# Output projections of tiles 3 and 4: input rows of the norm loaded one step ahead, first convolution rows into the weights' buffer

## The chip, the cores and the metric

The kernel runs on one core of one Trainium2 chip. TensorE (PE) multiplies matrices; VectorE (DVE) and ScalarE (ACT) do elementwise work, GpSimd (POOL) a little of it; SyncE (SP) issues most DMA transfers, ACT some. Engines run their own queues in order and wait for each other by semaphores. The metric is the device time of one execution in microseconds, and a kernel's time is the median of several runs.

## The reference, cut to what matters

One decoder layer on x (1 x 2048 x 1024, float32):

```python
hn = rms_norm(h, mix_pre_g)                  # h = x
proj = hn @ w_in
attn_out = sliding_window_attention(q, k, v, attn_sinks, rel_bias)   # window 128
conv_out = conformer_conv(u, ...)            # GLU, 31 taps, LayerNorm, swish, pointwise
mixed = jnp.concatenate([attn_out, conv_out], axis=-1) @ w_out
h = h + rms_norm(mixed, mix_post_g)          # output projection and its norm
hn = rms_norm(h, ffn_pre_g)
ff = (jax.nn.silu(hn @ w_gate) * (hn @ w_up)) @ w_down               # D_FF = 2816
h = h + rms_norm(ff, ffn_post_g)
```

The change lies in the fifth to seventh of these lines: the product with `w_out`, the norm behind it, the addition of the input x, and the norm ahead of the FFN.

## The kernel before, in words

Tokens are worked in four tiles of T = 512 (w = 0 to 3; "tiles 3 and 4" are w = 2 and 3). Float32 accuracy comes from splitting each operand into a high and a low part and multiplying three times; a split is one ACT copy and one DVE subtraction. Names in the trace are `tag@stage`: `ql@W` is a tile from the pool with tag `ql`, used in stage W. Stages of one letter with the tile's number: A input projection, B attention, C convolution, W output projection, N the norm behind W where it is a step of its own, H and F the FFN's gate and up projections (operands and products), G the FFN's down projection. F0 and G0 serve tiles 1 and 2 together, F2 and G2 tiles 3 and 4. The FFN uses a Strassen-like scheme: seven types of products, eleven pairs of blocks each, so G0 is 7 x 11 x 12 = 924 matmuls.

The program is built stage by stage, and a scheduler then orders each engine's queue. To fill gaps, stages run beside each other in lanes (generators that yield between portions of work). Beside G0 run, in this order: C2 (the convolution of tile 3), W2, C3, W3, and N3, the norm of W3; a second lane finishes the first FFN half. Then comes F2.

Every tag has a fixed number of buffers; a new tile waits until the oldest with that tag is no longer read or written. What matters here:

```python
BUFS = dict(x=4, p=4, wx=1, gb=2, hl=8, ql=4, chl=5, mid=4, mb=2, fa=4, at=2, fc=3, glu=2, yt=1, raw=2, w=6, vd=2)
```

`wx` is one buffer of 128 x 1024 float32, which early stages use for weights, the norm for a row block of x, and the finishing of the FFN (`ht`, L1149) for rows of h. `mid` has four buffers: the accumulators of W2 and W3 (`acc`), and later four operands of F2 (`mid@H`, split by ACT at L870 and DVE).

`stage_w` (from L723) is the output projection of one tile. It takes the eight blocks of `mixT` (attention and convolution results, transposed) in groups of two: `load(gi)` issues their DMAs (L749), `acts` splits them into `ql` (ACT L738, then DVE), `weight` loads and splits the weights (`w@W`, `raw@W`), and `block_half` multiplies (`tr@W`) and sums into `acc`. The first group is loaded when the stage begins. For tiles 3 and 4 blocks go to the two `at` buffers, that of w = 1 to a spare tile, and of w = 0 to `fa`.

`norm_w` (from L775) follows: squares of the four row blocks (s = 0 to 3), a factor by `rsqrt` (the `sm@W` chain), then per row block the scaling by factor and gain (`post_scale`, two DVE instructions per block, `mid@W<-mid@W,sm@W,gb@W`), the load of x rows (L798 into `wx` for one block, L804 in two halves for the others), the addition, the store of h to `h_scr` (L806) and the square (ACT L807). After the second factor ACT scales the blocks (L814) and stores them to `hn_scr` (L817). F2 reads columns of `hn_scr` back, transposes them (`tr@H`, L847) and splits them.

In G0 each step loads one operand (`fa@G` from `mids`, L1176; `at@G` in the first two steps) and one weight block (`mb@G`), splits both (`hl@G`, ACT L829 and DVE), and multiplies (`mm@G`). At the end of a type the sums leave PSUM through `p@G` (L1207, L1209), `mm@G` (L1249) and `x@G`.

Of the kernel before, what the change touches and what calls it, by code (L numbers as in the profile page):

```python
# [18 lines left out]
ALU = mybir.AluOpType  # L19
# [4 lines left out]
D = 1024  # L24
DFF = 2816
P = 128
T = 512
# [10 lines left out]
def layer_kernel(ctx, tc, x, xT, cols, rows, sinks, relb, onehot, w_in, w_pw, w_out, w_gate, w_up, w_down, out):  # L38
    nc = tc.nc
# [7 lines left out]
    lab = ["X0"]  # L47

    def nm(s):
        uid[0] += 1  # L50
        return f"{s}@{lab[0]}_{uid[0]}"
# [3 lines left out]
    def t_(tag, shape, dt=F32):  # L55
        return sb.tile(list(shape), dt, tag=tag, name=nm(tag), bufs=BUFS[tag])

    def f4(tag, shape=(P, D)):
        return t_(tag, shape)

    def f2(tag, shape=(P, T)):
        return t_(tag, shape)

    def hl(tag):
        return t_(tag, (P, 2, T), F32R)

    def sm(n, dt=F32):
        kind = "A" if lab[0][0] == "G" else lab[0][0]
        return sb.tile([P, 8], dt, tag="sm" + kind, name=nm("sm"), bufs={"C": 8, "W": 4}.get(kind, 16))[:, 0:n]
# [13 lines left out]
    def dve(op):  # L83
        def emit(*args, **kw):
            r = op(*args, **kw)  # L85
            if not paced[0]:
                pace["main"] = r.ins
            elif pace["main"] is not None and pace["main"] is not pace["tied"]:
                tc.add_manual_dep(
                    r.ins,  # L90
                    pace["main"].name,
                    mybir.DependencyInfo(mybir.DependencyClass.NoSync, mybir.DependencyReason.DATA),
                    reason="conv taps keep pace with the projections",
                )
                pace["tied"] = pace["main"]
            return r

        return emit

    stt = dve(nc.vector.scalar_tensor_tensor)  # L100
    vtt = dve(nc.vector.tensor_tensor)
# [38 lines left out]
    def weight(src, low, made, raw=None, on_pool=True):  # L140
        if raw is None:
            raw = t_("raw", (P, 2, T))
            nc.sync.dma_start(raw, src)
        return [split_w(raw[:, n], "w", low[n], made, on_pool) for n in range(2)]
# [5 lines left out]
    def rsqrt(ssq, n, mean_over, beside_taps=True):  # L150
        v = sm(n)
        y = sm(n)
        t = sm(n)
        vts(v, ssq, 1.0 / mean_over, EPS, ALU.mult, ALU.add)
        vts(y.bitcast(I32), v.bitcast(I32), 1, None, ALU.logical_shift_right)
        vts(y.bitcast(I32), y.bitcast(I32), -1, 0x5F3759DF, ALU.mult, ALU.add)
        for _ in range(3):
            if beside_taps:
                ptt(t, y, y, ALU.mult)
                ptt(t, t, v, ALU.mult)  # L160
                nc.gpsimd.tensor_scalar(t, t, -0.5, 1.5, ALU.mult, ALU.add)
                ptt(y, t, y, ALU.mult)
            else:
                vtt(t, y, y, ALU.mult)
                stt(t, v, -0.5, t, ALU.mult, ALU.mult)
                stt(y, t, 1.5, y, ALU.add, ALU.mult)
        return y
# [38 lines left out]
    for i in range(4):  # L206
        xt = f4("x", (P, 2, T))
# [415 lines left out]
    def spare_tile():  # L623
        if not spare:
            spare.append(t_("mb", (P, 2, T)))
        return spare[0]
# [76 lines left out]
    def block_half(acc, units, n, first, L, bank_of, s0=0):  # L703
        cs = slice(n * T, (n + 1) * T)
        for i in range(len(acc)):
            s = i + s0
            lab[0] = L
            o = bank_of()
            three(o, [((a[s // 4][:, 0, ss(s)], a[s // 4][:, 1, ss(s)]), (w[:, 0], w[:, 1])) for a, w in units])
            if first:  # L710
                act(acc[i][:, cs], o, AF.Copy)
            else:
                vtt(acc[i][:, cs], acc[i][:, cs], o, ALU.add)
            yield 0.65 * len(units)

    def load_gb(row):
        gb = []
        for n in range(2):
            t = f2("gb")
            nc.sync.dma_start(t, rows[row, n * T : (n + 1) * T].partition_broadcast(P))  # L720
            gb.append(t)
        return gb

    def post_scale(acc, gb, r):
        for n in range(2):
            cs = slice(n * T, (n + 1) * T)
            tied(stt(acc[:, cs], acc[:, cs], r, gb[n], ALU.mult, ALU.mult))

    def stage_w(w, spill, G, atag, htag, mtag, bank_of, norm=None):
        L = f"W{w}"  # L730
        lab[0] = L
        acc = [f4(atag) for _ in range(4)]

        def acts(gi, ms=None):
            aa = []
            for m in ms or load(gi):
                a = hl(htag)
                act(a[:, 0], m, AF.Copy)  # L738
                vtt(a[:, 1], m, a[:, 0].bitcast(F32), ALU.subtract)
                aa.append([a])  # L740
            return aa

        stage = spare_tile() if w == 1 else None

        def load(gi):
            ms = []
            for c in range(G * gi, G * gi + G):
                ms.append(stage[:, c % 2] if w == 1 else f2(mtag))
                nc.sync.dma_start(ms[-1], mixT[c, :, w * T : (w + 1) * T])  # L749
            return ms  # L750

        first = load(0)
        gb = load_gb(0) if w > 1 else None
        if w != 1:
            yield 5.0 if w == 0 else 8.0
            lab[0] = L
        nxt = acts(0, first)
        for gi in range(KC // G):
            aa = nxt
            for n in range(2):  # L760
                lab[0] = L
                if n == 0 and gi + 1 < KC // G:
                    if w < 2 and G * gi + G == 4:
                        ld.until(f"C{w}")
                        lab[0] = L
                    rows_next = load(gi + 1)
                if n == 1 and gi + 1 < KC // G:
                    nxt = acts(gi + 1, rows_next)
                src = w_out[2 * gi : 2 * gi + 2] if gi < 2 else w_join[2 * gi - 4 : 2 * gi - 2]
                ws = weight(src[:, :, n * T : (n + 1) * T].rearrange("c p t -> p c t"),  # L770
                            lo_out[n, 2 * gi : 2 * gi + 2], w > 0)
                yield from block_half(acc, list(zip(aa, ws)), n, gi == 0, L, bank_of)
        tail = norm_w(w, spill, acc, mtag, gb)
        if norm:
            norm(tail)  # L775
        else:
            yield from tail

    def norm_w(w, spill, acc, mtag, gb):
        L = f"W{w}"  # L780
        lab[0] = L
        gb = gb or load_gb(0)
        ssq = sm(4)
        for s in range(4):
            act(junk, acc[s], AF.Square, accum_out=ssq[:, s : s + 1])
            yield 0.5
            lab[0] = L
        r = rsqrt(ssq, 4, D, w < 3)
        yield 3
        lab[0] = L  # L790
        ssq2 = sm(4)
        for s in range(4):
            lab[0] = L
            post_scale(acc[s], gb, r[:, s : s + 1])
            r0 = w * T + s * P
            if s == (2 if mtag == "fa" else 0):
                xt = f4("wx")
                nc.sync.dma_start(xt, x[r0 : r0 + P])  # L798
                vtt(acc[s], xt, acc[s], ALU.add)
            else:  # L800
                for n in range(2):
                    cs = slice(n * T, (n + 1) * T)
                    xt = f2(mtag if s == 1 or w > 1 else "fa")
                    nc.sync.dma_start(xt, x[r0 : r0 + P, cs])  # L804
                    vtt(acc[s][:, cs], xt, acc[s][:, cs], ALU.add)
            nc.sync.dma_start(h_scr[r0 : r0 + P], acc[s])  # L806
            act(junk, acc[s], AF.Square, accum_out=ssq2[:, s : s + 1])  # L807
            yield 5.0
        lab[0] = L
        r2 = rsqrt(ssq2, 4, D, w < 3)  # L810
        yield 3
        lab[0] = L
        for s in range(4):
            act(acc[s], acc[s], AF.Copy, scale=r2[:, s : s + 1])  # L814
            if spill:
                r0 = w * T + s * P
                nc.scalar.dma_start(hn_scr[r0 : r0 + P], acc[s])  # L817
        yield 0.1
        hns[w] = acc
# [727 lines left out]
```

## Time and profile before

| | |
| --- | --- |
| times of three runs, us | 1981.5, 1977.93, 1981.22 |
| median, us | 1981.22 |
| profiled execution, us | 1986.73 |
| its span, us | 1984.7 |
| mean granted clock of TensorE in it | 0.992 |
| instructions | 26851 |

The profile is of one execution, which was 5.5 us over the median; its span is 2 us shorter than its own device time. The trace gives each instruction its start, its duration and, in square brackets, the engine's idle time before it with what ended that. In rows of groups, three durations are minimum, median and maximum in ns.

### The profile page before, as it was taken

Reading aid. Unit: us, or ns where it says so; the run is one execution under the profiler, and the core shown is the slowest. Engines: PE = TensorE matmul, PEld = TensorE weight load, DVE = VectorE, ACT = ScalarE, POOL = GpSimd, SP = SyncE. Lnnn points to the kernel's source line nnn. Section 1 sums busy time; section 2 is a strip of 40 time slices with the busy share of each in tenths; the row PEclk is TensorE's granted clock in tenths of the full one; section 3 lists DMA queues with packets and bytes.
Section 4 is the critical chain, followed back from the end, with each engine's and each line's share of the span. In section 5 each row is a group of like instructions: output and inputs, shape, how many; then the busy total and the mean of one; then the engine's idle time right before and its main releaser. Section 6 shows DMA issues by size and latency. Waiting matters only on the chain.

```text
span 1984.7 us, 26851 instructions
## 1 busy us (share of the span) xinstructions
PE 1937.4 (98%) x8730; PEld 1545.6 (78%) x8730; DVE 1493.7 (75%) x2679; ACT 969.5 (49%) x1910; POOL 335.2 (17%) x395
## 2 busy tenths in 40 slices
PE   9999999999999999989999999999999999999998
PEld 7877667677768878768878878777888888888886
DVE  5998989697793899888748995688766665455557
ACT  5455334546576633333345446477544433345443
POOL 6001212331120300000000011005423332311000
PEclk9999999999999999999999999999999999999999
DMA  8886646568758676686577778679745442366654
GB/s 313 275 308 224 203 149 186 181 193 305 270 166 303 224 252 223 230 275 233 193 241 252 226 270 276 215 291 345 265 142 176 170 153 91 136 224 202 212 190 155
DMA packets 229181, 443.56 MB, mean 223 GB/s; under 512 B 22920, under 2 KB 48688, under 8 KB 229040
## 3 DMA queue, kind: packets, MB, share of 16 engines
q1 hardware_dynamic: 207408, 406.19, 61.0%
q10 hardware_dynamic: 19392, 28.32, 3.9%
q0 software_dynamic: 2240, 7.34, 0.9%
q8 instruction: 68, 1.11, 0.2%
q14 instruction: 73, 0.60, 0.1%
HBM read 320.64 MB, written 121.12 MB: 223 GB/s over the span
## 4 chain that ended last, share of the span: by engine, by line
PE 77%; DVE 8%; DMA 8%; ACT 3%; issue 2%; POOL 1%; SPq 0%; ACTq 0%; DVEq 0%; POOLq 0%
PE mm@F L108 36%; PE mm@G L108 16%; PE mm@A L108 12%; PE mm@W L108 4%; PE tr@W L108 3%; PE tr@B L108 3%; DVE fc@C L85 3%; PE ct@J L108 1%; DMA raw@A<-w_in 1%; DVE mid@W L85 1%; DMA at@W<-mixT 1%; DMA gb@F<-keeps 1%; DMA mids<-fa@F 1%; DVE w@F L85 1%; DMA mixT<-fc@C 1%
## 5 line engine op out<-in xcount | busy, mean ns | idle before, releaser
L85 DVE SCALAR_TENSOR_TENSOR fc@C<-glu@C,colt,fc@C 128x512 f32<-128x512 f32 x480 | 365.9, 778 | 2.2
L108 PE MATMUL mm@F<-hl@H,w@F 128*128 128x512 f32 x1056 | 257.6, 392 | 3.5 <-ACT mm@F L983 3.5
L108 PEld LDWEIGHTS mm@F<-hl@H,w@F 128*128 128x128 f32 x1056 | 198.7, 189 | 48.4 <-ACT mm@F L983 4.8
L108 PE MATMUL mm@G<-hl@G,hl@G 128*128 128x512 f32 x924 | 226.0, 395 | 6.6 <-ACT mm@G L1249 2.2
L108 PE MATMUL mm@A<-hl@A,w@A 128*128 128x512 f32 x840 | 209.3, 399 | 2.1 <-DVE hl@A L85 1.1
L108 PEld LDWEIGHTS mm@G<-hl@G,hl@G 128*128 128x128 f32 x924 | 172.3, 189 | 45.5 <-ACT mm@G L1249 2.6
L108 PE MATMUL mm@G<-w@G,hl@G 128*128 128x512 f32 x876 | 199.5, 389 | 0.0
L829 ACT ACTIVATE w@F<-chl@F 128x512 fp32r<-128x512 f32 x220 | 134.7, 624 | 126.4 <-PE mm@F L108 119.3
L108 PEld LDWEIGHTS mm@G<-w@G,hl@G 128*128 128x128 f32 x876 | 164.4, 188 | 34.1
L108 PEld LDWEIGHTS mm@A<-hl@A,w@A 128*128 128x128 f32 x840 | 156.8, 190 | 40.6 <-issue 3.6
L85 DVE TENSOR_TENSOR w@F<-chl@F,w@F 128x512 fp32r<-128x512 f32 x198 | 143.3, 728 | 36.9 <-ACT w@F L829 36.4
L108 PE MATMUL mm@F<-ql@H,w@F 128*128 128x512 f32 x528 | 131.3, 392 | 7.2 <-ACT mm@F L1071 3.7
L108 PE MATMUL mm@F<-mid@H,w@F 128*128 128x512 f32 x528 | 131.3, 391 | 2.8 <-ACT fa@F L1092 2.6
L108 PE MATMUL mm@F<-p@H,w@F 128*128 128x512 f32 x528 | 131.2, 394 | 0.0
L108 PE MATMUL mm@F<-x@H,w@F 128*128 128x512 f32 x528 | 127.5, 390 | 0.0
L108 PEld LDWEIGHTS mm@F<-ql@H,w@F 128*128 128x128 f32 x528 | 98.6, 188 | 28.6 <-ACT mm@F L1071 4.6
L108 PEld LDWEIGHTS mm@F<-mid@H,w@F 128*128 128x128 f32 x528 | 98.6, 188 | 24.9 <-ACT fa@F L1092 3.5
L108 PEld LDWEIGHTS mm@F<-p@H,w@F 128*128 128x128 f32 x528 | 100.7, 191 | 21.6 <-ACT at@F L1085 0.3
L108 PEld LDWEIGHTS mm@F<-x@H,w@F 128*128 128x128 f32 x528 | 98.6, 188 | 21.3 <-DVE sm@B L460 0.8
L133 ACT ACTIVATE w@A<-raw@A 128x512 fp32r<-128x512 f32 x110 | 67.4, 626 | 77.4 <-PE mm@A L108 42.9
L108 PE MATMUL mm@W<-w@W,hl@W 128*128 128x512 f32 x384 | 103.2, 408 | 1.6 <-ACT fa@A L355 1.6
L85 DVE TENSOR_TENSOR w@G<-raw@G,w@G 128x512 fp32r<-128x512 f32 x73 | 51.5, 705 | 67.7 <-ACT w@G L829 66.7
(308 smaller groups left out, 3313.9 us busy)
## 6 DMA issues: line engine op xcount, KB each, us to landing
mids<-fa@F SPq DMA_DIRECT2D x154, 256.0 KB, 2.8
raw@A<-w_in SPq DMA_DIRECT2D x55, 512.0 KB, 4.7
w@A<-lo_in SPq DMA_DIRECT2D x84, 256.0 KB, 3.7
fc@G<-mids SPq DMA_DIRECT2D x77, 256.0 KB, 3.3
fa@G<-mids SPq DMA_DIRECT2D x75, 256.0 KB, 5.0
w@W<-lo_out SPq DMA_DIRECT2D x48, 256.0 KB, 4.1
chl@F<-w_gate SPq DMA_DIRECT2D x22, 512.0 KB, 4.2
raw@F<-w_gate SPq DMA_DIRECT2D x22, 512.0 KB, 3.7
```

What stands on the lines that cost most here:

```text
L85: r = op(*args, **kw)
L108: r = nc.tensor.matmul(*args, **kw)
L133: act(w[:, 0], raw, AF.Copy)
L829: act(w[:, 0], x, AF.Copy)
```

## The change

In `load`, the first group of tiles 3 and 4 (w > 1, gi = 0) goes into one tile of tag `wx`, shared by its two blocks, instead of two `at` tiles.

In `norm_w`, the loads of x rows move into a helper, `load_x_rows(s)`. For tiles 3 and 4 the rows of blocks 0 (in `wx`) and 1 (in `at`) are loaded ahead of the loop over the row blocks, and those of block s + 1 at the end of step s, from step 1 on. For tiles 1 and 2 a block's rows are loaded where they were. The addition of the block in `wx`, one DVE instruction over 1024 columns, becomes two over 512 in all four tiles.

```diff
         def load(gi):
             ms = []
+            pair_ = stage if w == 1 else t_("wx", (P, 2, T)) if w > 1 and gi == 0 else None
             for c in range(G * gi, G * gi + G):
-                ms.append(stage[:, c % 2] if w == 1 else f2(mtag))
+                ms.append(pair_[:, c % 2] if pair_ is not None else f2(mtag))
                 nc.sync.dma_start(ms[-1], mixT[c, :, w * T : (w + 1) * T])
             return ms
...
         r = rsqrt(ssq, 4, D, w < 3)
+        rows_x = {}
+
+        def load_x_rows(s):
+            if s < 4:
+                lab[0] = L
+                r0 = w * T + s * P
+                rows_x[s] = []
+                if s == (2 if mtag == "fa" else 0):
+                    xt = f4("wx")
+                    nc.sync.dma_start(xt, x[r0 : r0 + P])
+                    rows_x[s] = [xt[:, 0:T], xt[:, T:D]]
+                    return
+                for n in range(2):
+                    xt = f2(mtag if s == 1 or w > 1 else "fa")
+                    nc.sync.dma_start(xt, x[r0 : r0 + P, n * T : (n + 1) * T])
+                    rows_x[s].append(xt)
+
+        if w > 1:
+            load_x_rows(0)
+            load_x_rows(1)
         yield 3
...
             post_scale(acc[s], gb, r[:, s : s + 1])
             r0 = w * T + s * P
-            if s == (2 if mtag == "fa" else 0):
-                xt = f4("wx")
-                nc.sync.dma_start(xt, x[r0 : r0 + P])
-                vtt(acc[s], xt, acc[s], ALU.add)
-            else:
-                for n in range(2):
-                    cs = slice(n * T, (n + 1) * T)
-                    xt = f2(mtag if s == 1 or w > 1 else "fa")
-                    nc.sync.dma_start(xt, x[r0 : r0 + P, cs])
-                    vtt(acc[s][:, cs], xt, acc[s][:, cs], ALU.add)
+            if w < 2:
+                load_x_rows(s)
+            for n in range(2):
+                cs = slice(n * T, (n + 1) * T)
+                vtt(acc[s][:, cs], rows_x[s][n], acc[s][:, cs], ALU.add)
             nc.sync.dma_start(h_scr[r0 : r0 + P], acc[s])
             act(junk, acc[s], AF.Square, accum_out=ssq2[:, s : s + 1])
+            if w > 1 and s:
+                load_x_rows(s + 1)
             yield 5.0
```

Lines below the helper move down by 18 in the changed kernel (L829 becomes L847, L1176 becomes L1194). The counts of matmuls, ACT instructions and DMAs stay; DVE has four instructions more. The scheduler's order differs only in W0 and W1 (the two halves of one addition each) and from the end of F0 through G0 to the first products of F2, where all engines' queues are reordered around W2, C3, W3 and N3.

## The prediction

> **What bounds the kernel now.** I read the page first (span, busy times, the chain that ended last), then PE's busy time by stretches of 50 us where the change acts, then PE's waits in those 400 us, then the order of events around each wait. From the page:
>
> ```profile
> span 1984.7 us, 26851 instructions
> PE 1937.4 (98%) x8730; PEld 1545.6 (78%) x8730; DVE 1493.7 (75%) x2679; ACT 969.5 (49%) x1910; POOL 335.2 (17%) x395
> PE 77%; DVE 8%; DMA 8%; ACT 3%; issue 2%; POOL 1%; SPq 0%; ACTq 0%; DVEq 0%; POOLq 0%
> ```
>
> TensorE works for 98% of the span, and the change adds and removes no matmul. It can only create or remove idle time of PE. Outside the output projections of tiles 3 and 4 (labels W2 and W3), the instruction order of the changed kernel is that of before, but for two additions. W2 and W3 run beside G0, the down projection of tiles 1 and 2, from 1015 to 1340 us, so I asked for PE's time from 1000 to 1400 (the sum of eight windows) and for its waits there (total us, times, longest):
>
> ```profile
> sum 400.00, PE 389.27 PEld 317.76 DVE 311.61 ACT 233.50 POOL 54.65; mean PE 48.66 PEld 39.72 DVE 38.95 ACT 29.19 POOL 6.83
> PE tr@W L108 <- ACT ql@W L738: 2.5, 1, 2.5
> PE mm@G L108 <- ACT mm@G L1249: 2.2, 1, 2.2
> PE mm@G L108 <- DVE p@G L1209: 1.7, 1, 1.7
> PE tr@H L847 <- issue: 1.6, 1, 1.6
> PE mm@G L108 <- DVE x@G L85: 1.4, 1, 1.4
> PE mm@G L108 <- DVE hl@G L85: 0.7, 1, 0.7
> PE mm@G L108 <- ACT p@G L1207: 0.5, 1, 0.5
> ```
>
> PE is idle for 400.00 - 389.27 = 10.73 us here, all of it in seven waits (10.6 us). That is the most that any gain can be. A loss has no such cap.
>
> **Part 1: W2's first rows, loaded early into wx.** The 2.5 us wait is what this part meets. The order of time around it:
>
> ```profile
> 1014.70 1.52 PE L108 MATMUL mm@G<-hl@G,hl@G 128*128 128x512 f32 x6
> 1019.05 1.87 SPq L749 DMA_DIRECT2D at@W<-mixT  x2
> 1025.59 1.32 ACT L738 ACTIVATE ql@W<-at@W 128x512 fp32r<-128x512 f32 x2 [5.25 <-DMA at@W<-mixT]
> 1026.28 1.66 PE L108 MATMUL tr@W<-w@W,ql@W 128*128 128x512 f32 x6 [2.53 <-ACT ql@W L738]
> 1029.87 0.32 SPq L1176 DMA_DIRECT2D fa@G<-mids  x1
> 1033.19 5.74 PE L108 MATMUL tr@W<-w@W,ql@W 128*128 128x512 f32 x24
> 1038.77 1.98 PE L108 MATMUL mm@G<-hl@G,hl@G 128*128 128x512 f32 x8
> DMA to landing us min/median/max: 2.5/5.0/7.6
> ```
>
> The rows leave for SBUF at 1019.05, land after some 5 us, and PE waits 2.53. (The last line is the landing of fa@G, G0's reloaded operands.) In the changed order the two blocks load where the x row of tile 3 stood in SP's queue, long before; 15 of W2's products move ahead of F0's last 12, and 42 W2 products in all still stand ahead of G0's third operand pair, the first that comes from fa@G. So the question is when that pair is ready. One product costs 5.74 / 24 = 0.239 us. From 1014.70, 42 W2 products (10.0), 12 of F0 (2.9), the 24 of G0 (5.6) and the small transposes (about 1) end at 1034.2. The pair's load is issued at 1029.87, after stores of F0 whose own order in SP's queue stays; 5.0 to land and two splits of 0.66 and 0.69 give 1036.2. PE would then wait about 2.0 us, and F0's last products come 15 x 0.23 = 3.4 us later, which can delay those stores by up to another us. So 2.53 goes and 2 to 3 comes: **0**, bounds -2.5 (the reload lands at its minimum) and +1.0.
>
> The Trainium skill, "SBUF — State Buffer", section "The DMA setup-cost knee", fits a DMA's time as 2 us plus the bytes over 436 GB/s, which is an estimate of 2.6 us for these 256 KB; by it the pair would be ready before PE asks and part 1 would gain its 2.5 us. The median of 5.0 above disagrees, in a stretch where much else is in flight, and the sum goes by the row.
>
> **Part 2: x rows one step ahead, and tile 4's first rows in wx.** The norm of W2 runs at 1155 us, that of W3 near 1300:
>
> ```profile
> 1155.15 5.39 DVE L85 SCALAR_TENSOR_TENSOR mid@W<-mid@W,sm@W,gb@W 128x512 f32<-128x512 f32 x8 [2.05 <-POOL sm@W L162]
> 1304.66 1.34 DVE L85 TENSOR_TENSOR mid@W<-at@W,mid@W 128x512 f32<-128x512 f32 x2 [2.75 <-DMA at@W<-x]
> 1308.42 3.84 PE L108 MATMUL mm@G<-hl@G,hl@G 128*128 128x512 f32 x13 [1.37 <-DVE x@G L85]
> L85 DVE TENSOR_TENSOR mid@W<-wx@W,mid@W x3: 1218/1220/1222, 585.5 to 1296.5; 128x1024 f32<-128x1024 f32 x3
> L85 DVE TENSOR_TENSOR mid@W<-at@W,mid@W x14: 683/687/695, 601.7 to 1323.1; 128x512 f32<-128x512 f32 x14
> DMA at@W<-x: 6.3, 4
> ```
>
> At 1155 the eight scalings hold DVE for 5.39 us. The three waits of 1.7, 0.7 and 0.5 come from that block, not from the x rows: G0's evacuations and splits queue behind it. Its place among G0's splits is the same in both orders, so I keep them: 0. One addition of 1024 columns (1.220) becomes two of 512 (2 x 0.687 = 1.374), 0.15 us more for each of four tiles on DVE, 75% busy: 0, at most +0.6. The two new additions in tiles 1 and 2 lie where PE does not wait for DVE: 0.
>
> The additions of all norms wait 6.3 us for x rows (last line), and one such wait, 2.75 us at 1304.66, ends in PE's 1.4 us at 1308.42, because x@G's evacuation stands behind it on DVE. Loading a step ahead takes that 2.75 away. But the order shows what comes instead. Tile 4's last convolution block, whose taps share DVE, is transposed after 669 of G0's 924 products, against 625; W3's last product moves from behind G0's 702nd to its 736th. So the norm of W3 starts about 34 x 0.229 = 7.8 us later against G0, and its eight scalings (5.39 as above) now meet the evacuation of the fifth type of G0 blocks instead of lying ahead of it. At 1155 the same meeting cost 1.7 + 0.7 + 0.5 = 2.9; I take 2.7 here in place of 1.4: **+1.3**, bounds -1.4 (free) and +2.9. The 2.2 us wait behind the reloaded last mixT block of tile 4 stays, a chain of DMAs that moves with its taps: 0, bounds -1.5 and +1.5.
>
> **Part 3: what is late next.** W3's four accumulators (mid@W) are reused as operands of F2, the next stage. Ends of the two stages now:
>
> ```profile
> 1331.71 8.42 PE L108 MATMUL mm@G<-hl@G,hl@G 128*128 128x512 f32 x36
> 1333.61 2.18 ACT L814 ACTIVATE mid@W<-mid@W,sm@W 128x1024 f32<-128x1024 f32 x2
> 1338.13 0.69 DVE L1209 COPY p@G<-mm@G 128x512 f32<-128x512 f32 x1
> 1338.16 1.03 SPq L1149 DMA_DIRECT2D wx@G<-h_scr  x1
> 1340.33 5.74 PE L108 MATMUL mm@F<-ql@H,w@F 128*128 128x512 f32 x24
> 1340.73 0.63 ACT L870 ACTIVATE mid@H<-gb@H 128x512 fp32r<-128x512 f32 x1 [0.64 <-DMA hn_scr<-mid@W]
> 1345.35 0.75 DVE L85 SCALAR_TENSOR_TENSOR p@G<-p@G,sm@G,wx@G 128x512 f32<-128x512 f32 x1 [1.89 <-DMA wx@G<-h_scr]
> 1345.90 2.76 PE L108 MATMUL mm@F<-mid@H,w@F 128*128 128x512 f32 x10
> 1346.96 1.29 DVE L85 TENSOR_TENSOR mid@H<-gb@H,mid@H 128x512 fp32r<-128x512 f32 x2
> hn_scr<-mid@W ACTq DMA_DIRECT2D x12, 512.0 KB, 4.2
> ```
>
> The final scaling of W3 (L814) starts 6.7 us ahead of G0's end at 1340.33, its store frees a buffer, ACT and DVE split F2's operand mid@H into it, and PE reads it from 1345.90 with no stall to speak of. In the changed order the last step of the chain that gives L814 its factor stands on DVE behind the copy of a G0 bank that runs at 1338.13 here, and an addition of 0.69: L814 cannot start before about 1340, 6.5 us later. ACT's split of the first mid@H follows at about 1340.4 + 1.1 + 4.2 + 1 = 1346.7. On DVE the second split stands behind p@G<-...,wx@G, which waits for rows of h in the single wx buffer. That load leaves when the additions before it are done, some 1342 (1338.16 here), and takes 1345.35 - 1338.16 = 7.2: 1349. The additions and w@F work ahead of the second split take 2.9 us, those between the others about 4.5: splits 2 to 4 end near 1352.5, 1354.5 and 1357. PE's order is now 36 ql@H products, then all 24 of mid@H: it needs them from 1340.33 + 36 x 0.239 = 1348.9, six products (1.4) each, the fourth at 1353.2. Late by 1357 - 1353.2 = 3.8, and a little for splits that slip behind ACT: **+4.3**, bounds 0 (DVE's work ahead of the splits takes no longer than before, as 36 products cover it) and +6. Nothing else can fill: the banks of the products in flight are taken.
>
> The 1.6 us of tr@H L847 after that waits for columns loaded from hn_scr; while PE waits for mid@H these land: -0.8, bounds -1.6 and 0.
>
> **Sum.** 0 + 0 + 1.3 + 0 + 4.3 - 0.8 = +4.8 us. The profiled execution took 1986.73 us (span 1984.7), 5.5 over the median of 1981.22; the same sum on each gives 1991.5 for a profile and **1986.0** for the median. A measurement of this kernel tells about 0.2%, 4 us, from no change.
>
> **Rivals.** First, *the early rows simply pay*: faster. The 2.5 at 1026 goes and the fa@G pair is there by 1034; the 1.4 behind DMA at@W<-x goes, and the 1.6 at tr@H: -5.5, 1975.7. It decides if the fa@G reload lands in under 2.9 us from 1029.87 and the mid@H splits end by 1353. For it: at 1304.66 the wait on x rows is plain. Against: 5.0 is the median landing, and the order puts W3 later against G0. The Trainium skill, "DMA: Bandwidth & Descriptors", section "Rules for kernel authors", advises to issue a DMA early and to wait for it late, which speaks for this rival; the trace agrees at 1304.66 and, by fa@G, not at 1026.
>
> Second, *waits only change places*: part 1's stall is swapped, the 36 products ahead of mid@H cover its delay, the norm's collision costs what the removed wait gave: 0, 1981.2. For it: PE came out of all this at 98% busy, and DVE's slips are short.
>
> Third, *the shared buffer costs more*: the mid@H delay of 6, the full 2.9 at the fifth type and +1.0 in part 1: 6 + 2.9 + 1.0 = 9.9, 1991.1. The Trainium skill, "Trainium Kernel Development and Optimization", section "Best Practices", asks to double-buffer what DMA fills while engines compute, and wx has one buffer; the 1.89 at 1345.35 agrees. Tile 4's first rows must wait there until tile 3's first row is added, but their products stand behind 448 of G0's, well after that. That the edit does nothing is excluded: the order differs over the whole of G0.
>
> **Chances.** My sum 0.42 (1986.0), waits only move 0.30 (1981.2), rows pay 0.18 (1975.7), the dearer case 0.10 (1991.1). Faster by over 0.2% is the third of these, within it the second, slower the other two: 0.18, 0.30, 0.52. The range leaves out half of the faster case and a part of the dearest: 1976.5 to 1992.0; the forecast's own case spans 1982 to 1990.
>
> **What would show it.** In the new profile: PE's wait for ql@W near 1026 gone, and a wait of 2 to 3 us on hl@G<-fa@G near 1034; DVE's scalings of W3 near 1310 with a PE wait on p@G or x@G beside them; L814 of W3 starting after G0's end, and PE waiting 4 us for DVE mid@H some 10 us after it. I am wrong if mid@H is ready when PE comes to it, or if PE's idle time from 1000 to 1400 falls below 10.7.

## The result: slower by a quarter of a per cent, and the profile after

| | before | changed |
| --- | --- | --- |
| median of 18 runs each, us | 1983.12 | 1986.85 |
| lowest and highest, us | 1977.28, 1988.69 | 1983.13, 1996.88 |
| profiled execution, us | 1986.73 | 1989.83 |
| its span, us | 1984.7 | 1988.0 |

The ratio is 1.0026, with a 95% interval of 1.0015 to 1.0037: about 5.2 us slower, between 3.0 and 7.3; the two medians differ by 3.7. The forecast was 1986.0, +4.8 us. The profile page of the changed kernel, the lines that answer to those of before (span, busy times, the chain that ended last):

```profile
span 1988.0 us, 26848 instructions
...
PE 1936.9 (97%) x8730; PEld 1543.2 (78%) x8730; DVE 1488.0 (75%) x2683; ACT 970.8 (49%) x1910; POOL 334.9 (17%) x395
...
PE 69%; DVE 12%; DMA 11%; issue 3%; ACT 2%; POOL 1%; SPq 1%; DVEq 0%; ACTq 0%; POOLq 0%
```

PE is busy as long (1936.9 us against 1937.4) in a span 3.3 us longer, so the loss is idle time of PE. DVE and DMA have the larger shares of the chain. PE's time and waits from 1000 to 1400 us, as they were asked of before:

```profile
sum 400.00, PE 386.13 PEld 314.06 DVE 306.40 ACT 231.69 POOL 49.90; mean PE 48.27 PEld 39.26 DVE 38.30 ACT 28.96 POOL 6.24
```

```profile
PE mm@F L108 <- DVE mid@H L85: 3.7, 2, 3.3
PE mm@G L108 <- DVE hl@G L85: 3.6, 2, 2.9
PE tr@W L108 <- DVE mid@W L85: 1.7, 2, 0.9
PE mm@G L108 <- ACT hl@G L847: 1.0, 1, 1.0
PE mm@G L108 <- DVE x@G L85: 0.9, 1, 0.9
PE tr@H L865 <- issue: 0.8, 1, 0.8
...
```

Idle time rises from 10.73 to 400.00 - 386.13 = 13.87 us, which is 3.1 of the 3.3 us. The 2.5 on ql@W and the 2.2 on mm@G are gone; the largest new wait is for mid@H, at the start of F2. How it comes about, in order of time on ACT, DVE, SP and PE:

```profile
1336.55 2.19 ACT L832 ACTIVATE mid@W<-mid@W,sm@W 128x1024 f32<-128x1024 f32 x2 [0.24 <-DVE sm@W L85]
...
1337.28 5.74 PE L108 MATMUL mm@F<-ql@H,w@F 128*128 128x512 f32 x24
...
1340.95 0.93 SPq L1167 DMA_DIRECT2D wx@G<-h_scr  x1
...
1344.03 0.69 DVE L85 TENSOR_TENSOR mid@H<-gb@H,mid@H 128x512 fp32r<-128x512 f32 x1 [0.72 <-ACT mid@H L888]
...
1345.03 0.63 ACT L888 ACTIVATE mid@H<-gb@H 128x512 fp32r<-128x512 f32 x1
...
1346.38 1.97 PE L108 MATMUL mm@F<-mid@H,w@F 128*128 128x512 f32 x8
...
1347.45 1.63 DVE L85 SCALAR_TENSOR_TENSOR p@G<-p@G,sm@G,wx@G 128x512 f32<-128x512 f32 x1 [2.73 <-DMA wx@G<-h_scr]
...
1350.87 0.68 DVE L85 TENSOR_TENSOR mid@H<-gb@H,mid@H 128x512 fp32r<-128x512 f32 x1
...
1351.60 3.48 PE L108 MATMUL mm@F<-mid@H,w@F 128*128 128x512 f32 x12 [3.25 <-DVE mid@H L85]
...
1354.82 0.69 DVE L85 TENSOR_TENSOR mid@H<-gb@H,mid@H 128x512 fp32r<-128x512 f32 x1
...
1355.57 1.21 PE L108 MATMUL mm@F<-mid@H,w@F 128*128 128x512 f32 x4 [0.49 <-DVE mid@H L85]
```

ACT's half of the second mid@H is done at 1345.7. DVE's half waits in its queue behind p@G<-p@G,sm@G,wx@G, which itself waits 2.73 us for rows of h, loaded into the one wx buffer at 1340.95. The split runs at 1350.87, 5.2 us after ACT's half, and PE stands 3.25 us, and 0.49 again at the fourth. In the kernel before, the second split ran ahead of that addition (which came at 1345.35 there):

```profile
1341.39 0.69 DVE L85 TENSOR_TENSOR mid@H<-gb@H,mid@H 128x512 fp32r<-128x512 f32 x1
```

### The profile page after: what moved, and what is told of

It reads as the page before. It is cut to its first block, busy times and chain, and to the rows that moved or that the text cites. A ratio compares the mean times of both kernels' runs of the same rounds, so it can differ in the third digit from the quotient of the medians.

```text
span 1988.0 us, 26848 instructions
## 1 busy us (share of the span) xinstructions
PE 1936.9 (97%) x8730; PEld 1543.2 (78%) x8730; DVE 1488.0 (75%) x2683; ACT 970.8 (49%) x1910; POOL 334.9 (17%) x395
## 4 chain that ended last, share of the span: by engine, by line
PE 69%; DVE 12%; DMA 11%; issue 3%; ACT 2%; POOL 1%; SPq 1%; DVEq 0%; ACTq 0%; POOLq 0%
PE mm@F L108 30%; PE mm@G L108 15%; PE mm@A L108 11%; PE mm@W L108 4%; DVE fc@C L85 4%; PE tr@B L108 3%; PE tr@W L108 3%; DVE w@F L85 1%; DMA raw@A<-w_in 1%; PE ct@J L108 1%; DVE chl@F L85 1%; DMA td<-fc@G 1%; DMA mixT<-fc@C 1%; DVE hl@G L85 1%; DVE fa@F L85 1%
## 5 line engine op out<-in xcount | busy, mean ns | idle before, releaser
L847 ACT ACTIVATE w@F<-chl@F 128x512 fp32r<-128x512 f32 x220 | 134.7, 625 | 131.0 <-PE mm@F L108 121.0
```

Of the source, the lines that this page charges most:

```text
L847: act(w[:, 0], x, AF.Copy)
```

## What the change does to the program

A kernel built with the early loads of x rows as its only edit has, instruction by instruction and wait by wait on every engine, the program of the kernel before. The whole change has the program of a kernel with only its two other edits. So "one step ahead" is in the source and not in the program; the scheduler places those loads the same way wherever the source issues them. The effect is that of two edits: first rows of tiles 3 and 4 in wx, and the additions in halves.

## The experiments

Three theories. A: the loss is the late operand mid@H at F2's start; A1 holds that W3's late norm frees its buffers late, A2 that its splits stand on DVE behind additions that wait for h rows. B: the reuse of buffers and the extra work inside G0 cost. C: any new order of G0's queues costs some microseconds. "Us against before" below is the ratio's excess over one times 1984.

**The two edits, and the two tiles.** First the halves alone (no `pair_`, no early loads):

```diff
-                vtt(acc[s], xt, acc[s], ALU.add)
+                for n in range(2):
+                    cs = slice(n * T, (n + 1) * T)
+                    vtt(acc[s][:, cs], xt[:, cs], acc[s][:, cs], ALU.add)
```

> Only the additions in two halves; no rows in wx early. In its instruction order the norm of W3 begins behind the same share of G0's splits as before (126 of 154) and F2 starts with the same products. Theory A (the loss is W3's norm ending late, so that F2's operands mid@H come late): no wait for mid@H, within 1 us of the kernel before. Theory B (the extra work and the reuse of buffers inside G0 cost): +0.6 us from four additions of 0.15 us each. Theory C (any new order of G0's queues costs some us, whatever its cause): up to 4 us either way, with no wait for mid@H needed.

Measured 0.9985 (0.9969 to 1.0002): -3 us, at the edge of what can be told from none, and no wait for mid@H. B's +0.6 is not there; the halves are not the cost.

Then the first rows in wx for both tiles (`pair_` as in the change), with the addition whole and the x rows loaded where they were:

```diff
-                ms.append(stage[:, c % 2] if w == 1 else f2(mtag))
+                ms.append(pair_[:, c % 2] if pair_ is not None else f2(mtag))
```

> First rows of tiles 3 and 4 in wx, additions whole, x rows loaded where they were. W3's norm begins behind 130 of 154 splits (132 with the whole change, 126 before); F2's order is 24 ql@H, 3 mid@H, 12 ql@H, 15 mid@H. Theory A: the wait at 1026 falls by 1.5 us, a wait for mid@H of 2 to 4 us appears: +1 to +3 us. Theory B: the whole change's loss, +5 us, with the waits inside G0. Theory C: anything from -4 to +5.

Measured 1.0019 (1.0005 to 1.0034), +4 us: the early rows carry the loss. Its wait at F2's start:

```profile
1346.99 5.06 PE L108 MATMUL mm@F<-mid@H,w@F 128*128 128x512 f32 x14 [2.55 <-DVE mid@H L85]
```

It lies in the expected 2 to 4 us; the time is at the far side of theory A's +1 to +3. It is not the only loss of this trace: PE idles 5.4 us from 1300 to 1410, against 3.1 in before, but also 11.2 from 1020 to 1300, against 7.6, so this run doesn't exclude B. Now the whole change for one tile, by conditions `w == 2` and `w == 3` in place of `w > 1` (the additions stay in halves in all tiles):

> The whole change for tile 3 alone; tile 4's first rows in the at buffers as before. W3's norm begins latest of all, behind 136 of 154 splits, last product behind 762 of G0's 924. Theory A: the wait for mid@H is at least that of the whole change, 4 to 7 us, less 1.5 gained at 1026: +3 to +6 us. Theory B, with tile 4's sharing of wx as the cause: that is gone, so -1.5 to 0 us. Theory C: anything from -4 to +5.

> The whole change for tile 4 alone; tile 3's first rows in the at buffers, so the wait for ql@W near 1026 stays at 2.5 us. W3's norm begins behind 130 of 154 splits. Theory A: a wait for mid@H of 1 to 3 us: +1 to +3 us. Theory B: tile 4's sharing of wx costs, +5 us. Theory C: anything from -4 to +5.

Tile 3 alone: 1.0036 (1.0023 to 1.0050), +7 us. Tile 4 alone: 1.0024 (1.0008 to 1.0040), +5. Each is as dear as both together, so the parts do not add up. Two of PE's longest waits in each, late in G0 and in F2, tile 3 alone first (two lines), then tile 4 alone (two lines):

```profile
1304.28 1.11 PE L865 MATMUL tr@H<-ident,at@H 128*128 128x128 f32 x4 [2.98 <-ACT gb@H L885]
...
1349.97 3.47 PE L108 MATMUL mm@F<-mid@H,w@F 128*128 128x512 f32 x14 [2.62 <-DVE mid@H L85]
```

```profile
1265.18 0.73 PE L108 MATMUL mm@G<-hl@G,hl@G 128*128 128x512 f32 x2 [2.16 <-ACT mm@G L1267]
...
1360.47 0.66 PE L865 MATMUL tr@H<-ident,at@H 128*128 128x128 f32 x4 [2.20 <-DVE chl@H L85]
```

Theory A asked for 4 to 7 us of mid@H with tile 3 alone; it has 2.62, though W3's norm comes latest there, and pays elsewhere. With tile 4 alone only 1.27 us is left, on ACT's half of mid@H, and a wait for chl@H stands beside it. A as "the later the norm, the longer the wait" falls. B's claim that sharing wx with tile 4 is what costs falls too, since tile 3 alone costs as much. C is borne out this far: each order has its own waits.

**Buffers or queue?** The change as it is was run again beside three variants.

> The changed kernel as it is, to stand beside the next three on one chip. +3 to +7 us against before, with the wait for mid@H of 3 to 4 us at the start of F2.

1.0022 (1.0009 to 1.0035), +4.4 us, with the same wait:

```profile
1354.34 3.47 PE L108 MATMUL mm@F<-mid@H,w@F 128*128 128x512 f32 x12 [3.24 <-DVE mid@H L85]
```

Next F2's operands B21 leave W3's accumulators:

```diff
-        2: dict(B11=["ql"] * 4, B21=["mid"] * 4, T1=["hl"] * 4, ...
+        2: dict(B11=["ql"] * 4, B21=["hl"] * 4, T1=["mid"] * 4, ...
```

> The change, with F2's operands B21 in four hl buffers instead of W3's mid accumulators (T1, which is needed later, takes those). All queues of G0 keep the changed kernel's order around W2, C3, W3 and N3. Theory A (W3's late norm holds the buffers of mid@H): the wait for that operand, 3.25 and 0.49 us, goes; -3 to -4 us against the change, +1 to +2 against before. Theory C (any new order costs, this is only where it shows): the operand's wait may go, but the time stays within 1.5 us of the change's.

Measured 1.0031 (1.0015 to 1.0046), nothing won. The rows of DVE and PE (the operand is hl@H here):

```profile
1327.14 0.68 DVE L85 TENSOR_TENSOR hl@H<-gb@H,hl@H 128x512 fp32r<-128x512 f32 x1
...
1346.04 1.83 DVE L85 SCALAR_TENSOR_TENSOR p@G<-p@G,sm@G,wx@G 128x512 f32<-128x512 f32 x1 [4.92 <-DMA wx@G<-h_scr]
...
1349.05 0.68 DVE L85 TENSOR_TENSOR hl@H<-gb@H,hl@H 128x512 fp32r<-128x512 f32 x1
...
1349.78 7.39 PE L108 MATMUL mm@F<-hl@H,w@F 128*128 128x512 f32 x20 [3.96 <-DVE hl@H L85]
```

In other buffers, free of W3, the first split comes 8 us ahead of G0's end (1335.59 here), where it came 7 us after it in the change. But the second is as late as ever: it ends 14.1 us after G0's end, against 14.3. A1 falls. ACT's half of it was done at 1342.9; DVE waits 4.92 us for h rows, and the split stands behind.

The same exchange on the kernel before:

> The kernel before with the same exchange of buffers. There was no wait for mid@H to take away. Theory A: within 1.5 us of before. Theory C: up to 4 us either way, since F2's queues are reordered.

0.9993 (0.9977 to 1.0010): no effect, as expected of a kernel without that wait.

Then the h rows into the `raw` buffers, to take their wait away:

```diff
-            ht = f4("wx" if L == "G0" else "mid")
+            ht = f4("raw" if L == "G0" else "mid")
```

> The change, with the rows of h for the finishing of G0 in the two raw buffers instead of the one wx buffer, so that the vector queue at G0's end does not wait for them; F2's operands stay in W3's accumulators. Theory A1 (the buffers are freed late by W3's norm): a wait for mid@H of 2 to 4 us stays, +3 to +6 against before. Theory A2 (the splits stand behind additions that wait for h rows in wx): the wait goes, 0 to +2 against before.

1.0180 (1.0160 to 1.0200), +36 us. No wait for mid@H is left, but this tells nothing of A2: another wait came first and buried it, PE's for columns of F2's operands:

```profile
1356.62 1.09 PE L865 MATMUL tr@H<-ident,fc@H 128*128 128x128 f32 x4 [13.81 <-DMA fc@H<-hn_scr]
```

**Taking the h rows out, and changing precedence.** Left out are the loads of h and, with them, the residual h of tiles 1 and 2; the gain rows at hand are added in its place:

```diff
-                stt(halves[n], halves[n], r[:, j : j + 1], ht[:, cs], ALU.mult, ALU.add)
+                stt(halves[n], halves[n], r[:, j : j + 1], gb[n], ALU.mult, ALU.add)
```

> The change, where the finishing of G0 adds the gain rows at hand instead of loading rows of h: it leaves out the residual h of tiles 1 and 2, and eight loads of 512 KB, with as many DVE instructions. G0's order around W2, C3, W3 and N3 is the changed kernel's; W3's accumulators still hold mid@H's buffers. Theory A2 (the splits of mid@H stand on DVE behind additions that wait for h rows in the one wx buffer): the wait of 3.2 us for mid@H goes, under 1 us is left, and the time is 3 to 4 us under the change's, about before's. Theory A1 (buffers): the wait stays at 2 to 4 us. Theory C (order alone): the wait may go, but the time stays at +3 to +6.

> The same edit on the kernel before; it too leaves out the residual h of tiles 1 and 2. Before had no wait for mid@H, so theory A2 expects -1 to +1 us against before, and 0 to 3 us less than the run with the change. Theory C: up to 4 us either way.

1.0084 (1.0064 to 1.0104) on the change, 1.0020 (1.0002 to 1.0039) on before: leaving work out made both slower. Before's +4 is within C's 4 us; the change's +17 is outside what any of the theories gave. On the change the wait for mid@H did not go:

```profile
1349.96 0.75 DVE L85 SCALAR_TENSOR_TENSOR p@G<-p@G,sm@G,glu@G 128x512 f32<-128x512 f32 x1 [1.47 <-POOL sm@G L162]
...
1352.62 0.69 DVE L85 TENSOR_TENSOR mid@H<-gb@H,mid@H 128x512 fp32r<-128x512 f32 x1
...
1353.36 2.08 PE L108 MATMUL mm@F<-mid@H,w@F 128*128 128x512 f32 x4 [3.64 <-DVE mid@H L85]
```

Without the loads the scheduler put more of the finishing ahead of the fourth split, which now stands behind an addition that waits for POOL. ACT's half of it was done at 1348.15. This run misses A2's numbers, and its 3.64 us lies in A1's 2 to 4; but the trace again shows a split late by its place in DVE's queue, not by its buffer. PE's longest waits here are others (7.5 us in two for DVE's fa@F), and part of this trace's loss is no wait but the granted clock, 0.94 from 1300 to 1410 us against 1.00 in the change: PE is busy 1944.0 us in all, against 1936.9.

The last edit keeps all work and gives the lane of F2's operands precedence, from B21 on, in every engine's queue:

```diff
+    lh.lag = -150
     lh.add("B21.2", stage_h_plain(ws, ops, "B21", 4), lambda: since(lw, "N3", NS))
```

> The change, with the lane that makes F2's operands given precedence: on DVE the second split of mid@H now stands ahead of the additions that wait for h rows (2, 2, 4 and 4 of those additions ahead of the four splits, as in the kernel before; 2, 4, 4, 4 with the change). G0's order is the changed kernel's. Theory A2: the wait shrinks to 0 to 2 us, time 2 to 3 us under the change's. Theory A1: the wait stays. Theory C: +3 to +6 against before.

1.0006 (0.9991 to 1.0020), +1 us against before. Against the change's 1.0026 and 1.0022 that is 3 to 4 us won. With intervals of 0.0011 to 0.0015 to either side of each, that is at the edge of what can be told from nothing, so more rests on the trace. DVE and PE in it:

```profile
1341.38 0.69 DVE L85 TENSOR_TENSOR mid@H<-gb@H,mid@H 128x512 fp32r<-128x512 f32 x1
...
1343.61 0.76 DVE L85 SCALAR_TENSOR_TENSOR p@G<-p@G,sm@G,wx@G 128x512 f32<-128x512 f32 x1 [1.54 <-DMA wx@G<-h_scr]
...
1348.01 2.60 PE L108 MATMUL mm@F<-mid@H,w@F 128*128 128x512 f32 x10 [0.94 <-DVE mid@H L85]
```

The second split now stands ahead of the addition that waits for h, and PE's wait falls from 3.25 to 0.94. The stretch from 1300 to 1410 us (width, PE busy, then the other engines) in before, the change, the change again, and this run, one fence each:

```profile
1300.00:1410.00 110.00, 106.91 (x490) 87.17 (x490) 90.97 (x156) 77.66 (x150) 40.65 (x45) 1.00 0.94 328
```

```profile
1300.00:1410.00 110.00, 102.91 (x470) 82.97 (x469) 85.86 (x156) 76.42 (x148) 32.36 (x42) 1.00 0.90 309
```

```profile
1300.00:1410.00 110.00, 103.41 (x472) 83.34 (x472) 87.17 (x159) 76.51 (x149) 29.74 (x41) 1.00 0.89 306
```

```profile
1300.00:1410.00 110.00, 107.86 (x496) 88.17 (x495) 90.40 (x157) 78.92 (x155) 41.19 (x46) 1.00 0.95 329
```

PE idles 3.1 us in before, 7.1 and 6.6 in the change, 2.1 with the precedence: 3.5 to 4.0 us of the loss lie here. The other order gives back 4.5 to 5.0, 2.8 of it from the wait for mid@H, the rest from shorter waits of F2. That is A2, tried from both ends (other buffers: nothing won; other order: won). The second test is not of one instruction, though: ACT's half of the first mid@H also came earlier, 3.2 us after G0's end against 6.1, and PE's products were reordered.

> No rows in wx early, only the additions in two halves, and the same precedence for F2's operands. No wait for mid@H expected. If halves and precedence add up: -2 to -4 us against before, the best version; theory C: up to 4 us either way.

Last, the halves with the precedence and no early rows: 0.9993 (0.9974 to 1.0012). The two do not add up to a version that can be told from before. None of the twelve beat it beyond doubt; the halves alone came nearest.

## Why the prediction held, and where it did not

The direction was right, and so were the main place of the loss and its mechanism on DVE. **Part 3, F2's start: +4.3 forecast, 3.7 measured** (PE's waits for mid@H, in the change and in its repeat). W3's final scaling began 0.7 us ahead of G0's end (1336.55 against 1337.28); I had said about at it, against 6.7 in before. The second to fourth splits were to end 12.2, 14.2 and 16.7 us after G0's end; in the trace the second ended at 1351.55, 14.3 after it, and the fourth at 1355.51, 18.2. The wait I put at the fourth fell mostly on the second, for the reason that Part 3 named on DVE: the split stands behind the addition that waits for h rows in wx. Those rows were there 10.2 us after G0's end, against 8.7 forecast. The other half of that step was not it: it told the chain from L814 by way of the freed buffers as well, and in the run with other buffers the wait stayed. That 1.6 us at tr@H became 0.8, as forecast, is luck: the old wait (28.6 us after G0's end) went altogether, and the 0.8 is another, 45.4 us after it. With the precedence, where PE hardly waits for mid@H, the old one is gone as well, so the reason given for it is not shown.

**Part 1: forecast 0, measured about -1.2.** A wait on fa@G came in place of that on ql@W, as said, but shorter:

```profile
1027.22 1.49 SPq L1194 DMA_DIRECT2D fa@G<-mids  x2
...
1033.34 0.63 ACT L847 ACTIVATE hl@G<-fa@G 128x512 fp32r<-128x512 f32 x1 [3.65 <-DMA fa@G<-mids]
...
1034.02 2.37 PE L108 MATMUL mm@G<-hl@G,hl@G 128*128 128x512 f32 x9 [0.98 <-ACT hl@G L847]
```

The failed step is the issue time. I held the load at 1029.87; it left at 1027.22. Landing took some 6 us against my 5.0, and PE's first product needed the high half alone, not both splits. One trace is a poor measure of such a wait: in the eight traces with tile 3's rows early it was 0.98 to 2.04 us, 1.55 on average, and in six with them in at (the wait on ql@W) 1.55 to 3.85, 2.75 on average. So the gain is some 1.2 us. The Trainium skill's fit from "SBUF — State Buffer", section "The DMA setup-cost knee", 2.6 us for such a load, is again too short for this stretch: from 1027.22 to 1033.34 it took 6.1. The load of at@W that PE waited for in before also took longer than the "some 5 us" that I read there, 6.5 from 1019.05 to 1025.59.

**Part 2: forecast +1.3 and 0, measured otherwise.** Three steps failed. W3's norm did come later, 8.8 us against G0's end (7.8 forecast), but its eight scalings did not meet the evacuation of the fifth type; they ran from 1295.73, and PE's wait there fell from 1.4 to 0.95:

```profile
1295.73 5.39 DVE L85 SCALAR_TENSOR_TENSOR mid@W<-mid@W,sm@W,gb@W 128x512 f32<-128x512 f32 x8
...
1305.99 2.34 PE L108 MATMUL mm@G<-hl@G,hl@G 128*128 128x512 f32 x9 [0.95 <-DVE x@G L85]
```

I also wrote that loading a step ahead takes the 2.75 us wait on x rows away. That edit changed nothing in the program, so whatever shortened the wait, it was not that. The third is the norm of W2, which I had put at 0. PE's three waits there, 2.9 us in before and in both of its variants with the same G0 order, became 4.1, most of it one wait for a split:

```profile
1161.43 2.49 PE L108 MATMUL mm@G<-hl@G,hl@G 128*128 128x512 f32 x6 [2.91 <-DVE hl@G L85]
```

In the five other traces with this order of G0 they are 3.5 to 6.1; what lengthens them was not taken apart. The 2.2 us wait behind tile 4's last block, put at 0 within 1.5, went in this trace and in its repeat, and stayed at 2.16 with tile 4 alone.

A term was missing: PE waits for DVE to empty the banks of W2's and W3's products, which it did not in before.

```profile
1080.71 1.28 DVE L85 TENSOR_TENSOR mid@W<-mid@W,tr@W 128x512 f32<-128x512 f32 x2
...
1081.44 0.73 PE L108 MATMUL tr@W<-w@W,ql@W 128*128 128x512 f32 x2 [0.88 <-DVE mid@W L85]
```

With the like wait of 0.82 at 1269.97 that is 1.7 us, and 2.6 in the run with B21 in hl (the halves alone have 0.7). Together these sizes roughly cancel in G0: from 1020 to 1300 us PE idled 7.6 us in before and 9.3 in before with B21 exchanged, against 6.8, 11.7, 9.3 and 10.5 in the change, its repeat, and the runs with B21 in hl and with precedence. That is some 1 us on average, less than one trace differs from the next, and it stays open. So is the cost of each tile alone, whose waits are scattered and were not taken apart further. That the sum, +4.8, came so near the measured +5.2 is therefore partly luck: Part 3 earned most of it, and the errors of Parts 1 and 2 (some 1.2, 1.8 and 2.2 us less than put down, 1.2 and 1.7 more) and F2's other new waits of 0.2 to 0.5 us largely cancel.

**The rivals.** That the early rows pay did not happen, since fa@G took part of the 2.5 and F2's start all of the rest. That waits only change places is near the truth inside G0 and wrong at F2. The dearer case did not come either: the wait for mid@H was 3.7, not 6, and the one at the fifth type fell. The Trainium skill's rule from "Trainium Kernel Development and Optimization", section "Best Practices", to double-buffer what DMA fills, fits what delayed DVE: the 2.73 us at 1347.45 is for a load that left at 1340.95, when the single wx had been read (until 1340.92). The try to give it two other buffers cost more elsewhere.

## What to carry to other kernels

Look past the wait that an edit removes to the start of the next stage: here what cost was not the moved transfer but one operand's place in an in-order queue, behind an instruction that waits for a DMA. Where a scheduler orders the queues, compare the instruction orders of the built programs before costing an edit; half of this one was not there, and moving work early elsewhere rearranged 300 us. Here the wait followed its operand into another buffer, so the buffer was not its cause; its place in the queue was the next thing to try.

## What was not expected

Leaving out work made the kernel slower: without the loads of h, the kernel before lost 4 us and the change, already 4 to 5 behind, stood 17 behind, while the order of the rest changed; why it cost that much was not taken apart. And the same order of G0 gave PE between 6.1 and 11.7 us of idle time from 1020 to 1300 us in five traces (the change, its repeat, B21 in hl, without h rows, with precedence), so single waits of 1 to 2 us in one trace there are not evidence on their own.
